# A QKV product on one core: second pair of row tiles loaded, cast and turned one tile at a time, and three smaller reorderings of the opening

## The chip, the core and the metric

The kernel runs on one core of one Trainium2 chip. The metric is the device time of one execution in microseconds, as the median of several runs. The core has TensorE (matrix products; the profile shows its products as PE and its loads of weights as PEld), VectorE (DVE), ScalarE (ACT), GpSimd (POOL) and SyncE (SP, which issues most of the transfers). SBUF is the working memory on the chip, PSUM holds the results of TensorE in eight banks per partition, and the inputs and outputs lie in HBM.

## The reference

```python
def setup_inputs():
    batch, seq, hidden = 16, 512, 768
    return {
        "x": np.random.randn(batch, seq, hidden).astype(np.float32),
        "w_qkv": np.random.randn(hidden, 3 * hidden).astype(np.float32),
    }

def reference(x, w_qkv):
    qkv = np.matmul(x, w_qkv)
    hidden = x.shape[-1]
    q = qkv[..., :hidden]
    k = qkv[..., hidden:2*hidden]
    v = qkv[..., 2*hidden:]
    return np.stack([q, k, v], axis=0).astype(np.float32)
```

It is one product of an 8192 x 768 matrix with a 768 x 2304 matrix, whose columns are split into three outputs.

## The kernel before

**Tiling.** The 8192 rows of x are taken in 32 pairs of row tiles of 128 rows each (`NP` is 32; "pair 0" is the first). The contraction of 768 is cut into six steps of 128 (`KT` 6), named j, or two halves of three steps (`KH` 3). The 2304 columns of w are cut into four blocks of 512 (`CB`) and a remainder of 256 (`REM`). Two blocks make a group q; group 0 holds columns 0 to 1023, group 1 columns 1280 to 2303, and the remainder lies between them.

**Two ways to multiply.** For most pairs, a pair of row tiles and a group of two blocks form a "quad": a 2 x 2 by 2 x 2 block product, done in seven products instead of eight (`product` and `do`, numbered 1 to 7). Products 1 and 2 use bf16 copies (`xb` of x, `b1` of w); products 3 to 7 use sums and differences in fp32r (`s` of x, made in `sums_x`; `t1` to `t4` of w, made by `sum_w`; and `b22`, a rounded copy of the last quarter of w). Pairs 0 and 1 come before these sums exist. Their blocks of columns are multiplied directly in bf16 by `block`, which runs over steps j and over the four row tiles 0 to 3 (tiles 0 and 1 are pair 0, 2 and 3 pair 1). `block(0, 0, ...)` uses the first 512 columns, `block(0, 1, ...)` the second 512. The list `singles` gives the order of j and tiles of the first of these.

**The order is written by hand.** Each engine executes its instructions in the order in which the program issues them, and waits for semaphores where it needs another engine's result. A DMA issued by SP waits until the eighth one before it has landed, so up to eight are on their way. They are taken from one queue in order.

**The opening.** The loads are issued in this order: x of pair 0 (768 KB), x of pair 1 (768 KB), six slices of w's first block (256 KB each, one for each j), w's second block in two transfers of 768 KB, a first part of x of pair 2, the remainder of w (768 KB), the seven other parts of pair 2 (96 KB each), then the blocks of group 1. TensorE first runs ten products of zeros (`busy(10)`, L469). `cast_rows` (by way of `copy_halves`, L165 and L166) rounds a pair's x to bf16, half of each row tile on VectorE and half on ScalarE. `turn_rows` then transposes it on TensorE (L185), six 128 x 128 turns to a row tile, and copies the result out of PSUM (L192 on ScalarE, L194 on VectorE) into `xb`. `cast_j` rounds one 512-column slice of w (L474 on ScalarE, L476 on VectorE). The products of `block` are L496, and its results are copied out of PSUM on ScalarE by the functions that it returns (`late`, L488).

**Pairs 2 and 3.** From pair 2 on, x comes in an order in which VectorE can turn it by itself (`transpose`, L155, in two halves for pairs 2 and 3: first the first row tile, then the second). `round_row` (L214 on ScalarE, L216 on GpSimd) rounds one row tile of a turned pair to bf16, and `sums_x` makes its five sums. After `block(1, 0, ...)` the copies of its results run on ScalarE; then come `sum_w(1, 1)`, `sum_w(1, 2)` (L119), the rounding of `b22[1]` on GpSimd (L621), the turning of pair 3, the rounding of its two row tiles, and its sums. `block(1, 1, ...)` follows. Pair 2's second quad `u2` then runs its products 1 and 2; products 1 of pair 3's two quads follow in `two`; and then `middle(u2)` adds product 6 into the bank that held u2's product 1. That bank has first been copied out by ScalarE (`evacuate`, L267). The products of the quads are L258, those with the remainder of w L321.

**The rest.** A loop takes two pairs at a time (`summed`, `plain`), with loads and turning of later pairs placed between the products. The change doesn't touch it.

Of the kernel before, what the change touches and what calls it, by code (L numbers as in the profile page):

```python
# [10 lines left out]
def kernel(  # L11
# [20 lines left out]
    nc = tc.nc  # L32
    P = 128
# [3 lines left out]
    K = H  # L37
    N3 = w_qkv.shape[1]
    KT = K // P
    KH = KT // 2  # L40
# [8 lines left out]
    bf16 = mybir.dt.bfloat16  # L49
    ident = mybir.ActivationFunctionType.Identity  # L50
# [3 lines left out]
    x_flat = x.rearrange("b t h -> (b t) h")  # L54
# [12 lines left out]
    xb_pool = ctx.enter_context(tc.tile_pool(name="xb", bufs=4))  # L67
    rem_pool = ctx.enter_context(tc.tile_pool(name="rem", bufs=1))
    s_pool = ctx.enter_context(tc.tile_pool(name="s", bufs=2))
    ps_pool = ctx.enter_context(tc.tile_pool(name="ps", bufs=8, space=bass.MemoryType.PSUM))  # L70
# [4 lines left out]
    eye = w_pool.tile([P, 176], bf16, name="eye")[:, :P]  # L75
    w_rem = [w_pool.tile([P, KH, REM], bf16, name="w_rem0"), None]

    b1 = [w_pool.tile([P, KT, CB], bf16, name=f"b1_{q}") for q in range(2)]
# [11 lines left out]
    def load_w(dst, j0, nj, off, cols):  # L90
        rows = w_qkv.rearrange("(p j) n -> p j n", j=KT)
        nc.sync.dma_start(dst, rows[:, j0:j0 + nj, off:off + cols])

    stage = {}

    def load_blocks(q, c, nj=KH):
        if q == 0:
            t = tq_pool.tile([P, KT, CB], fp32, name="st0", tag="tq")
            for j in range(0, KT, nj):
                load_w(t[:, j:j + nj], j, nj, Q_OFF[q] + c * CB, CB)  # L100
            stage[q, 0, c], stage[q, 1, c] = t[:, :KH, :], t[:, KH:, :]
        else:
            for h in range(2):
                if c == 0 and h == 0:
                    t = st_first
                else:
                    t = st_pool.tile([P, KH, CB], fp32, name="st1", tag="st")[:]
                load_w(t, h * KH, KH, Q_OFF[q] + c * CB, CB)
                stage[q, h, c] = t

    def sum_w(q, n):
        t1, t2, t3, t4 = ts[q]
        o, in0, in1 = {
            1: (t1, stage[q, 0, 1], stage[q, 0, 0]),
            2: (t2, stage[q, 1, 1], t1),
            3: (t3, stage[q, 1, 1], stage[q, 0, 1]),
            4: (t4, stage[q, 1, 0], t2),
        }[n]
        nc.vector.tensor_tensor(o, in0, in1, op=sub)  # L119

    xin, xf, xb, sr = {}, {}, {}, {}
# [25 lines left out]
    def transpose(p, parts=1, which=None):  # L147
        if p not in xf:
            xf[p] = xf_pool.tile([P, KT, 2 * P], fp32, name="xf")
        turned = xf[p][:].rearrange("p j (g b) -> p g j b", b=G)  # L150
        rows = xin[p][:].rearrange("p g (a j) -> p g j a", a=G)
        n = 2 * P // G // parts
        for i in range(parts) if which is None else (which, ):
            g = i * n
            nc.vector.transpose(turned[:, g:g + n], rows[:, g:g + n])  # L155

    def load_rows(p):
        xin[p] = xin_pool.tile([P, 2, K], fp32, name="xin")  # L160
        rows = x_flat[p * 2 * P:(p + 1) * 2 * P, :]
        nc.sync.dma_start(xin[p][:], rows.rearrange("(r m) k -> m r k", m=P))  # L162

    def copy_halves(dst, src):
        nc.vector.tensor_copy(out=dst[0], in_=src[0])  # L165
        nc.scalar.activation(dst[1], src[1], ident)  # L166

    xc = {}

    def cast_rows(p):  # L170
        src = xin.pop(p)
        xc[p] = s_pool.tile([P, 2, K], bf16, name="xc", tag="s")
        for r in range(2):
            halves = (slice(0, K // 2), slice(K // 2, K))
            copy_halves([xc[p][:, r, n] for n in halves], [src[:, r, n] for n in halves])

    def turn_rows(p, between=None):
        c = xc.pop(p)
        xb[p] = xb_pool.tile([P, KT, 2 * P], bf16, name="xb", tag="xb")
        turned = []  # L180
        for r in range(2):
            cols = c[:, r, :].rearrange("m (p j) -> m j p", j=KT)
            ps = ps_pool.tile([P, KT, P], bf16, name="ps")
            for j in range(KT):
                nc.tensor.transpose(ps[:, j, :], cols[:, j, :], eye)  # L185
            turned.append(ps)

        def copy(r, h, eng):
            n = slice(h * KH, (h + 1) * KH)
            dst, src = xb[p][:, n, r * P:(r + 1) * P], turned[r][:, n, :]  # L190
            if eng is nc.scalar:
                eng.activation(dst, src, ident)  # L192
            else:
                eng.tensor_copy(out=dst, in_=src)  # L194

        for r in range(2):
            copy(r, 0, nc.vector)
        if between is not None:
            between()
        for r in range(2):  # L200
            copy(r, 1, nc.scalar)

    def round_x(p):
        xb[p] = xb_pool.tile([P, KT, 2 * P], bf16, name="xb", tag="xb")
# [2 lines left out]
    act, dve = nc.scalar, nc.vector  # L207

    def round_row(p, r, eng):
        n = slice(r * P, (r + 1) * P)  # L210
        if r == 0:
            xb[p] = xb_pool.tile([P, KT, 2 * P], bf16, name="xb", tag="xb")
        if eng is act:
            eng.activation(xb[p][:, :, n], xf[p][:, :, n], ident)  # L214
        else:
            eng.tensor_copy(out=xb[p][:, :, n], in_=xf[p][:, :, n])  # L216

    def sums_x(p, eng=None):
        t = xf[p]
        a11, a12 = t[:, :KH, :P], t[:, KH:, :P]  # L220
        a21, a22 = t[:, :KH, P:], t[:, KH:, P:]
        s = s_pool.tile([P, 5, KH, P], f32r, name="s")
        sr[p] = s
        sums = {
            1: lambda g: g.tensor_tensor(s[:, 1], a21, a22, op=add),  # L225
            2: lambda g: g.tensor_tensor(s[:, 2], s[:, 1], a11, op=sub),  # L226
            3: lambda g: g.tensor_tensor(s[:, 3], a11, a21, op=sub),  # L227
            0: lambda g: g.tensor_copy(out=s[:, 0], in_=a22),
            4: lambda g: g.tensor_tensor(s[:, 4], a12, s[:, 2], op=sub),  # L229
        }  # L230
        if eng is not None:
            return sums
        for n in (1, 2, 3, 0, 4):
            sums[n](nc.gpsimd)
# [5 lines left out]
    def quad(p, q, pool=o_pool, tag="o"):  # L240
        u = Quad()
        u.p, u.q = p, q
        u.o = pool.tile([P, 2, 2 * CB], fp32, name="o", tag=tag)
        u.x = u.y = u.z = None
        return u
# [205 lines left out]
    zero = xb_pool.tile([P, CB], bf16, name="zero", tag="xb")  # L451
    nc.vector.memset(zero[:], 0.0)
    load_rows(0)
    nc.scalar.activation(tiny[:], zero[:, :1], ident)
    make_identity(nc, eye)
    load_rows(1)
    load_blocks(0, 0, 1)
    load_blocks(0, 1)
    st_rem = o_pool.tile([P, KT, REM], fp32, name="str", tag="o")
    load_x_rows(2, (0, ))  # L460
    load_w(st_rem[:], 0, KT, R_OFF, REM)
# [3 lines left out]
    def busy(n):  # L465

        ps = bank()
        for _ in range(n):
            nc.tensor.matmul(ps[:], zero[:, :P], zero[:], start=True, stop=True)  # L469

    def cast_j(q, c, w, j, eng=act):
        src = stage[q, j // KH, c][:, j % KH, :]
        if eng is act:
            eng.activation(w[:, j, :], src, ident)  # L474
        else:
            eng.tensor_copy(out=w[:, j, :], in_=src)  # L476
# [55 lines left out]
            round_x(p)  # L532
            sums_x(p)

    singles = [((0, ), (0, 1)), ((1, ), (0, 1)), ((0, 1), (2, 3))]
    singles += [((j, ), range(4)) for j in range(2, KT)]

    busy(10)
    cast_rows(0)
    turn_rows(0, lambda: cast_rows(1))  # L540
    busy(2)
    cast_j(0, 0, b1[0], 0, dve)
    cast_j(0, 0, b1[0], 1, dve)
    turn_rows(1)
    for j in range(2, KT):
        cast_j(0, 0, b1[0], j, dve)
    late0 = block(0, 0, b1[0], singles)
# [70 lines left out]
        f()  # L618
    sum_w(1, 1)
    sum_w(1, 2)  # L620
    nc.gpsimd.tensor_copy(out=b22[1][:], in_=stage[1, 1, 1])  # L621
    transpose(3, 2)
    round_row(3, 0, act)
    round_row(3, 1, nc.gpsimd)
    sums_x(3)
    sum_w(1, 3)
    sum_w(1, 4)
# [25 lines left out]
    for p in range(ND + 3, NP - 1, 2):  # L653
# [16 lines left out]
        c, d = quad(p + 1, 0), quad(p + 1, 1)  # L670
# [34 lines left out]
```

## Time and profile before

| What | Value |
|---|---|
| Time, median of 3 runs | 358.84 us (358.75 to 359.02) |
| Time of the profiled execution | 358.81 us |
| Its span, first to last instruction | 357.0 us |
| PE busy | 350.6 us, 98% of the span, 1757 instructions |
| DVE busy | 264.4 us, 74% |
| ACT busy | 185.0 us, 52% |
| POOL busy | 177.3 us, 50% |
| DMA moved | 108.10 MB, mean 303 GB/s |
| Granted TensorE clock, mean | 1.000 |

Times in the profile are microseconds from the first instruction. The span is what the profile covers; the device time of the same execution is 1.8 us longer. A busy engine is one that has an instruction in progress, and products on PE overlap each other, so "busy" alone doesn't say that nothing could start sooner. A timeline row gives the start, the duration, the engine and line, the operation, the tile written and the tiles read, the shape, and how many instructions were merged; in brackets stands the idle time before it and what ended that. PEld rows are loads of weights: a load is done shortly ahead of its product. The letter q after an engine's name means that engine's sequencer.

### The profile page before, as it was taken

Reading aid. Unit: us, or ns where it says so; the run is one execution under the profiler, and the core shown is the slowest. Engines: PE = TensorE matmul, PEld = TensorE weight load, DVE = VectorE, ACT = ScalarE, POOL = GpSimd, SP = SyncE. Lnnn points to the kernel's source line nnn. Section 1 sums busy time; section 2 is a strip of 40 time slices with the busy share of each in tenths; the row PEclk is TensorE's granted clock in tenths of the full one; section 3 lists DMA queues with packets and bytes.
Section 4 is the critical chain, followed back from the end, with each engine's and each line's share of the span. In section 5 each row is a group of like instructions: output and inputs, shape, how many; then the busy total and the mean of one; then the engine's idle time right before and its main releaser. Section 6 shows DMA issues by size and latency. Waiting matters only on the chain.

```text
span 357.0 us, 5315 instructions
## 1 busy us (share of the span) xinstructions
PE 350.6 (98%) x1757; PEld 252.1 (71%) x1776; DVE 264.4 (74%) x310; ACT 185.0 (52%) x317; POOL 177.3 (50%) x184
## 2 busy tenths in 40 slices
PE   7999999999999999999999999999999999999996
PEld 3474677768677686877768677686877768677674
DVE  3789876796877869777695877869777695876743
ACT  4587754545454553645545454553645545454553
POOL 0031773376566453665535566353665535566320
PEclk9999999999999999999999999999999999999999
DMA  7997999999999898998979899698999979887497
GB/s 296 380 353 238 325 378 340 373 317 348 308 311 340 257 361 206 347 266 285 361 197 385 227 342 307 209 402 213 347 263 307 331 196 392 225 303 280 155 380 260
DMA packets 82075, 108.10 MB, mean 303 GB/s; under 512 B 4992, under 2 KB 62080, under 8 KB 82048
## 3 DMA queue, kind: packets, MB, share of 16 engines
q1 hardware_dynamic: 75088, 102.52, 85.7%
q10 hardware_dynamic: 6960, 5.24, 5.5%
q8 instruction: 14, 0.23, 0.3%
q14 instruction: 13, 0.11, 0.1%
HBM read 32.24 MB, written 75.50 MB: 302 GB/s over the span
## 4 chain that ended last, share of the span: by engine, by line
PE 74%; POOL 15%; DVE 6%; issue 3%; DMA 2%; ACT 0%; SPq 0%
PE ps L258 56%; PE ps L321 12%; PE ps L496 6%; DVE xf L155 6%; POOL xb L205 5%; POOL s L226 3%; POOL s L225 3%; POOL s L227 3%; DMA xin<-in_x_dram 2%; PE ps L185 0%; DVE o L304 0%; ACT xc L166 0%; SPq L162 0%; DVE orem L424 0%; ACT orem L423 0%
## 5 line engine op out<-in xcount | busy, mean ns | idle before, releaser
L258 PE MATMUL ps<-t,s 128*128 128x512 f32 x720 | 177.9, 395 | 0.0
L258 PEld LDWEIGHTS ps<-t,s 128*128 128x128 f32 x720 | 135.1, 188 | 29.5
L155 DVE STREAM_TRANSPOSE xf<-xin 128x768 f32<-128x768 f32 (+1 forms) x45 | 93.3, 2075 | 4.3 <-DMA xin<-in_x_dram 4.3
L258 PE MATMUL ps<-b,xb 128*128 128x512 bf16 x343 | 81.6, 379 | 1.1
L298 DVE TENSOR_TENSOR o<-o,ps 128x512 f32<-128x512 f32 x56 | 38.5, 688 | 50.7 <-ACT o L297 50.0
L205 POOL CAST xb<-xf 128x1536 bf16<-128x1536 f32 x28 | 41.1, 1467 | 56.9 <-DVE xf L155 54.8
L225 POOL TENSOR_TENSOR s<-xf 128x384 fp32r<-128x384 f32 x29 | 31.0, 1068 | 72.9 <-DVE xf L155 71.1
L258 PEld LDWEIGHTS <-xb 128*128 128x128 bf16 x360 | 33.9, 98 | 36.7 <-issue 3.9
L304 DVE TENSOR_TENSOR o<-o,ps 128x512 f32<-128x512 f32 x60 | 41.1, 687 | 20.5 <-PE ps L258 19.4
L297 ACT ACTIVATE o<-ps 128x512 f32<-128x512 f32 x56 | 33.5, 598 | 42.1 <-PE ps L258 42.1
L258 PE MATMUL ps<-b,s 128*128 128x512 f32 x180 | 50.6, 389 | 0.0
L301 ACT ACTIVATE o<-ps 128x512 f32<-128x512 f32 x60 | 35.9, 598 | 25.2 <-PE ps L258 22.8
L378 DVE TENSOR_TENSOR o<-o,ps 128x512 f32<-128x512 f32 x78 | 47.8, 680 | 0.0
L321 PE MATMUL ps<-w_rem,xb 128*128 128x256 bf16 x384 | 47.4, 273 | 0.0
L286 ACT ACTIVATE o<-ps 128x512 f32<-128x512 f32 x60 | 35.9, 599 | 19.4 <-PE ps L258 14.0
L321 PEld LDWEIGHTS <-xb 128*128 128x128 bf16 x384 | 37.3, 98 | 11.5 <-issue 0.5
L335 ACT ACTIVATE orem<-ps 128x512 f32<-128x512 f32 x31 | 18.5, 598 | 48.3 <-PE ps L321 34.0
L258 PEld LDWEIGHTS ps<-b,s 128*128 128x128 f32 x180 | 33.8, 188 | 7.0
L226 POOL TENSOR_TENSOR s<-s,xf 128x384 fp32r<-128x384 f32 x29 | 29.5, 1018 | 2.3
L227 POOL TENSOR_TENSOR s<-xf 128x384 fp32r<-128x384 f32 x29 | 29.4, 1015 | 0.0
L229 POOL TENSOR_TENSOR s<-xf,s 128x384 fp32r<-128x384 f32 x29 | 29.2, 1008 | 0.0
L382 ACT ACTIVATE o<-ps 128x512 f32<-128x512 f32 x26 | 15.5, 598 | 17.9 <-PE ps L258 17.3
(49 smaller groups left out, 161.2 us busy)
## 6 DMA issues: line engine op xcount, KB each, us to landing
out_dram<-o SPq DMA_DIRECT2D x60, 768.0 KB, 4.6
out_dram<-o SPq DMA_DIRECT2D x75, 256.0 KB, 3.8
xin<-in_x_dram SPq DMA_DIRECT2D x88, 192.0 KB, 5.6
out_dram<-orem SPq DMA_DIRECT2D x31, 256.0 KB, 2.2
xin<-in_x_dram ACTq DMA_DIRECT2D x24, 192.0 KB, 4.4
st<-in_w_qkv_dram SPq DMA_DIRECT2D x5, 768.0 KB, 7.9
xin<-in_x_dram SPq DMA_DIRECT2D x2, 768.0 KB, 4.9
st<-in_w_qkv_dram SPq DMA_DIRECT2D x6, 256.0 KB, 6.0
```

What stands on the lines that cost most here:

```text
L155: nc.vector.transpose(turned[:, g:g + n], rows[:, g:g + n])
L205: nc.gpsimd.tensor_copy(out=xb[p][:], in_=xf[p][:])
L225: 1: lambda g: g.tensor_tensor(s[:, 1], a21, a22, op=add),
L226: 2: lambda g: g.tensor_tensor(s[:, 2], s[:, 1], a11, op=sub),
L227: 3: lambda g: g.tensor_tensor(s[:, 3], a11, a21, op=sub),
L258: nc.tensor.matmul(ps[:], lhs[j], rhs[j], start=(start and j == 0), stop=(j == KH - 1), skip_group_check=True,)
L286: nc.scalar.activation(c12, u.x[:], ident)
L298: nc.vector.tensor_tensor(c22, c22, u.y[:], op=add)
L301: nc.scalar.activation(c21, u.x[:], ident)
L304: nc.vector.tensor_tensor(c12, c12, u.y[:], op=add)
L321: nc.tensor.matmul(ps, xb[p][:, j, r * P:(r + 1) * P], w_rem[j // KH][:, j % KH, :], start=(j == 0), stop=(j == KT - 1), skip_group_check= ...
L378: dve.tensor_tensor(c, c, u.z[:], op=add)
```

## The change

Four things are changed, all before the loop.

1. Pair 1's x is loaded by two transfers of 384 KB, one for each row tile, where it was one of 768 KB. Casting and turning go by row tile: the first tile of pair 1 is cast and turned while the second is still on its way. The two filler products (`busy(2)`) stand between the two turns of pair 1.
2. The first slice of w (j = 0) is cast by VectorE (288 columns) and ScalarE (224 columns) where VectorE did it alone. `singles` is shorter: steps j are taken one at a time, j = 0 with tiles 0 and 1, then with tiles 2 and 3, then each other j with all four.
3. w's second block is loaded in six slices of 256 KB, where it was two transfers of 768 KB.
4. Pair 3's first row tile is rounded on GpSimd, ahead of the rounding of `b22[1]`, and its second on ScalarE; before, the first was rounded on ScalarE and the second on GpSimd, after `b22[1]`.

SP issues five more transfers in all; ScalarE gets its part of the first slice and one more copy of turned rows (the first half of the second tile of pair 1); and the order on VectorE changes as the code says.

```diff
-    def load_rows(p):
+    def load_rows(p, parts=(slice(0, 2), )):
         xin[p] = xin_pool.tile([P, 2, K], fp32, name="xin")
-        rows = x_flat[p * 2 * P:(p + 1) * 2 * P, :]
-        nc.sync.dma_start(xin[p][:], rows.rearrange("(r m) k -> m r k", m=P))
...
+        rows = x_flat[p * 2 * P:(p + 1) * 2 * P, :].rearrange("(r m) k -> m r k", m=P)
+        for r in parts:
+            nc.sync.dma_start(xin[p][:, r], rows[:, r])
+
+    xc, turned_rows = {}, {}
+
+    def cast_row(p, r):
+        if p not in xc:
+            xc[p] = s_pool.tile([P, 2, K], bf16, name="xc", tag="s")
+        dst, src = xc[p][:, r], xin[p][:, r]
+        nc.vector.tensor_copy(out=dst[:, :K // 2], in_=src[:, :K // 2])
+        nc.scalar.activation(dst[:, K // 2:], src[:, K // 2:], ident)
+
+    def turn_row(p, r):
+        if r == 0:
+            xb[p] = xb_pool.tile([P, KT, 2 * P], bf16, name="xb", tag="xb")
+        cols = xc[p][:, r, :].rearrange("m (p j) -> m j p", j=KT)
+        ps = ps_pool.tile([P, KT, P], bf16, name="ps")
+        for j in range(KT):
+            nc.tensor.transpose(ps[:, j, :], cols[:, j, :], eye)
+        turned_rows[p, r] = ps
+
+    def copy_row(p, r, h, eng):
+        n = slice(h * KH, (h + 1) * KH)
+        dst, src = xb[p][:, n, r * P:(r + 1) * P], turned_rows[p, r][:, n, :]
+        if eng is nc.scalar:
+            eng.activation(dst, src, ident)
+        else:
+            eng.tensor_copy(out=dst, in_=src)
...
-    load_rows(1)
+    load_rows(1, range(2))
     load_blocks(0, 0, 1)
-    load_blocks(0, 1)
+    load_blocks(0, 1, 1)
...
-    singles = [((0, ), (0, 1)), ((1, ), (0, 1)), ((0, 1), (2, 3))]
-    singles += [((j, ), range(4)) for j in range(2, KT)]
+    singles = [((0, ), (0, 1)), ((0, ), (2, 3))]
+    singles += [((j, ), range(4)) for j in range(1, KT)]
 
     busy(10)
-    cast_rows(0)
-    turn_rows(0, lambda: cast_rows(1))
+    for r in range(2):
+        cast_row(0, r)
+    for r in range(2):
+        turn_row(0, r)
+    cast_row(1, 0)
+    copy_row(0, 0, 0, dve)
+    copy_row(0, 1, 0, dve)
+    copy_row(0, 0, 1, act)
+    turn_row(1, 0)
     busy(2)
-    cast_j(0, 0, b1[0], 0, dve)
+    cast_row(1, 1)
+    turn_row(1, 1)
+    copy_row(1, 0, 0, dve)
+    k0, part = stage[0, 0, 0][:, 0, :], 288
+    dve.tensor_copy(out=b1[0][:, 0, :part], in_=k0[:, :part])
+    act.activation(b1[0][:, 0, part:], k0[:, part:], ident)
+    copy_row(1, 1, 0, act)
     cast_j(0, 0, b1[0], 1, dve)
-    turn_rows(1)
+    for p, r in ((0, 1), (1, 0), (1, 1)):
+        copy_row(p, r, 1, act)
     for j in range(2, KT):
         cast_j(0, 0, b1[0], j, dve)
...
     sum_w(1, 1)
     sum_w(1, 2)
+    transpose(3, 2)
+    round_row(3, 0, nc.gpsimd)
     nc.gpsimd.tensor_copy(out=b22[1][:], in_=stage[1, 1, 1])
-    transpose(3, 2)
-    round_row(3, 0, act)
-    round_row(3, 1, nc.gpsimd)
+    round_row(3, 1, act)
     sums_x(3)
```

More of the change, by code (lines that the diff above doesn't have):

```diff
@@ L155, in transpose @@
             nc.vector.transpose(turned[:, g:g + n], rows[:, g:g + n])
-    def load_rows(p):
+    def load_rows(p, parts=(slice(0, 2), )):
         xin[p] = xin_pool.tile([P, 2, K], fp32, name="xin")
-        rows = x_flat[p * 2 * P:(p + 1) * 2 * P, :]
-        nc.sync.dma_start(xin[p][:], rows.rearrange("(r m) k -> m r k", m=P))
[L164 to L201, printed above, removed]
+        rows = x_flat[p * 2 * P:(p + 1) * 2 * P, :].rearrange("(r m) k -> m r k", m=P)
```

## The prediction

> **What bounds the kernel now.** I read the stretches first (columns: stretch and length in us, then busy time of PE, PEld, DVE, ACT and POOL, granted clock, DMA share, GB/s).
>
> ```profile
> 0.00:8.00 8.00, 6.18 (x31) 2.69 (x32) 2.68 (x8) 3.50 (x7) 0.70 (x6) 1.00 0.76 283
> 8.00:21.00 13.00, 12.95 (x76) 7.07 (x77) 9.89 (x15) 7.03 (x14) 2.62 (x2) 1.00 1.07 366
> 21.00:46.00 25.00, 24.82 (x126) 14.38 (x127) 22.76 (x20) 20.26 (x39) 10.36 (x8) 1.00 0.92 309
> 46.00:343.00 297.00, 295.99 (x1478) 220.20 (x1491) 223.78 (x261) 148.85 (x249) 163.61 (x169) 1.00 0.92 300
> ```
>
> From 8 us on TensorE is busy for practically all of every stretch. A shift that TensorE still has at 46 us reaches the end; nothing after 46 us is changed. So I need two things: how early the products begin, and which instructions up to 46 us would make TensorE wait if it came earlier. Next the chain of waits over the opening, then the timeline of VectorE, ScalarE and TensorE there:
>
> ```profile
> 1.24 5.67 DMA xin<-in_x_dram
> ...
> 6.93 0.53 ACT xc L166
> ...
> 7.51 0.95 PE ps L185 x12
> 8.46 2.82 PE ps L496 x13
> ```
> ```profile
> 4.97 0.94 ACT L166 ACTIVATE xc<-xin 128x384 bf16<-128x384 f32 x2 [2.74 <-DMA xin<-in_x_dram]
> ...
> 6.93 0.63 DVE L165 CAST xc<-xin 128x384 bf16<-128x384 f32 x2
> ...
> 7.57 0.43 DVE L476 CAST b<-st 128x512 bf16<-128x512 f32 x1
> ...
> 8.26 0.43 DVE L476 CAST b<-st 128x512 bf16<-128x512 f32 x1 [0.27 <-DMA st<-in_w_qkv_dram]
> 8.29 5.36 PE L496 MATMUL ps<-b,xb 128*128 128x512 bf16 x23
> ```
>
> The second pair lands at 6.91, is cast, and its twelve turns (7.51 to 8.46) stand in TensorE's order ahead of the first product at 8.29. From there products follow each other every 0.216 us. Later, two places have no slack:
>
> ```profile
> 18.62 3.17 DVE L155 STREAM_TRANSPOSE xf<-xin 128x768 f32<-128x768 f32 x2 [0.78 <-DMA xin<-in_x_dram]
> ...
> 20.27 0.84 ACT L214 ACTIVATE xb<-xf 128x768 bf16<-128x768 f32 x1 [0.96 <-DVE xf L155]
> ...
> 21.18 0.42 PEld L258 LDWEIGHTS <-xb 128*128 128x128 bf16 x3
> ```
> ```profile
> 31.74 1.47 POOL L621 CAST b<-st 128x1536 fp32r<-128x1536 f32 x1 [8.92 <-DMA st<-in_w_qkv_dram]
> 31.78 3.03 DVE L119 TENSOR_TENSOR t<-st,t 128x1536 fp32r<-128x1536 f32 x1 [0.81 <-DMA st<-in_w_qkv_dram]
> ...
> 34.74 3.02 DVE L155 STREAM_TRANSPOSE xf<-xin 128x768 f32<-128x768 f32 x2
> ...
> 36.79 0.88 ACT L214 ACTIVATE xb<-xf 128x768 bf16<-128x768 f32 x1
> ...
> 37.52 2.09 ACT L488 ACTIVATE o<-ps 128x512 f32<-128x512 f32 x4
> ...
> 39.43 1.16 ACT L267 ACTIVATE o<-ps 128x512 f32<-128x512 f32 x2
> ```
>
> Place A: pair 2's first rows land at about 18.5, are turned on VectorE and rounded on ScalarE until 20.27 + 0.84 = 21.11; the load of weights that reads them starts at 21.18. Release to load takes 0.05 elsewhere (cast ends 7.46, turn starts 7.51), so the slack is 0.02. Place B: ScalarE has no idle time from 32.35 on. Its first L267 copy (0.67) ends at 40.10 and frees the bank into which `middle(u2)` accumulates; that load of weights starts at 40.15, so the slack is nothing. In ScalarE's order the rounding at 36.79 stands ahead of four copies and this one.
>
> **The change, part by part.**
>
> *Second pair by row tile.* The load of 768 KB landed 1.96 after the first pair's (4.97 to 6.93), so its first half should land at about 5.95. ScalarE's cast (0.52) ends at 6.49 and six turns run to about 7.1. The second half still lands at 6.91; its ScalarE cast ends at 7.46, and now six turns, not twelve, follow: 7.51 to 7.88, where the next load of weights can start. VectorE does its half casts and copies (0.28 to 0.36 each) in between, with the first pair's copies now behind the cast at 5.97 (they end near 6.9 instead of 6.89), before the 6.93 cast: no cost. The two fillers (L469) move between the two turns.
>
> *First slice cast by two engines.* Slice 0 starts its cast at 7.57, 0.01 after VectorE is free, and so has landed by then. VectorE's 288 of 512 columns take about 0.30 (384 take 0.36, 512 take 0.43), to 7.87; ScalarE's 224 take about 0.38 (384 take 0.52, 512 take 0.63), to 7.95. First product near 8.00 instead of 8.29: a gain of 0.29. What can now be late is the fourth row tile's copy, queued on ScalarE behind this part: 8.08 + 0.48 + 0.05 = 8.61 for a product due at 8.65, so at most 0.02 is lost. Slice 1 (cast 8.26 + 0.43 = 8.69) is now due at 8.87, the later ones land every 0.65 and are used every 0.86. Gain at the end of block one: 0.27 to 0.29.
>
> *Second block by slices.* Six transfers of 256 KB for two of 768 KB, and one more for the second pair: five more on SP's queue, which go past pair 2's rows, the remainder of w and all later loads. SP issues one in 0.44; slices use up 0.65 each, so issuing is no limit. SP is held by the landing of the eighth transfer before; that is now smaller, but eight of 256 KB still cover some 5 us. Is a small transfer slower? Slices 1 and 5 of block one are cast at 8.26 and 10.85, 0.65 a slice; the two 768 KB loads are cast at 12.77 and 14.88, so (14.88 - 10.85) / 6 = 0.67 for as much. Hence pair 2's rows land where they did; bounds 6 x 0.05 = 0.3 either way. The first slice of block two lands near 11.5 and not 12.75, so that block can start at 13.2. The waits behind these slices on ScalarE (slices 1, 3, 5, due at 14.1, 15.8, 17.5) have a microsecond or more.
>
> The Trainium skill, in DMA: Bandwidth & Descriptors, section Bandwidth, has the rule to batch transfers to 1 MiB or more for three quarters of the peak, and its section on one DMA's anatomy gives a constant cost of about 2.0 us for each; five more, were that not overlapped, would be 10 us by an estimate from that page. The rows of 0.65 and 0.67 above do not agree with it here.
>
> What the first three parts give is taken back at place A: TensorE arrives up to 0.29 earlier, but pair 2's rows are bound by their landing. What is left is 0.02.
>
> *Pair 3's rounding.* Before, GpSimd's b22 cast (31.74) held VectorE's subtraction beside it: 3.03 for what takes 1.75 at 29.22. It now comes after row 0's rounding, so that subtraction should end at 31.78 + 1.75 = 33.53. The turning of pair 3 then waits for its first four parts; the fourth landed at 33.87, 7.5 us after its issue at 26.36. With the 0.12 that passed at place A between landing and start, it runs from 34.0 and both halves (3.03 together) end at 37.02. GpSimd rounds row 0 at about 35.6 to 36.4 (half of L205's 1.47), long before it is needed (the seventh of twelve loads of weights that begin at 37.55, one every 0.216: 38.85); b22 follows to 37.8 and is needed at 42.88 (PEld row). It may hold the next subtraction by 0.8, which was held elsewhere before (2.38 at 39.32), and whose result is needed at 42.30 (PEld row): nothing. But ScalarE's rounding now is of row 1, the second half: it starts at 37.05 and not at 36.79. Everything behind it moves by 0.26, the copies and then place B: load of weights at 40.42 instead of 40.15. The 0.02 is lost in this wait too, since ScalarE's chain doesn't depend on it. If the rows land up to 0.3 off, the chain before them (held by a store in the same queue) moves along, so I take 0.27 with bounds 0 and 0.6.
>
> **Sum.** -0.29 at the start, + 0.27 at place A, + 0.29 at place B (the 0.02 that was still ahead, and 0.27 beyond the old time): the end is 0.27 later. Profiled execution: span 357.0 + 0.3 = 357.3, time 358.81 + 0.27 = 359.08; the median is 0.03 above it, so 359.1. That is 0.07%, while about 0.2% (0.72 us) is what a measurement can tell from no change.
>
> **The rivals.**
>
> *No wait at B.* If ScalarE's copies catch up, or the second half is turned by 36.75, only place A counts: 358.84 - 0.02 = 358.8. For it: ScalarE's rate behind the rounding is that of its own work. Against: no idle time to catch up in.
>
> *The start's gain survives.* It needs pair 2's rows 0.25 earlier and B clear: 358.84 - 0.28 = 358.56. Against: DMA share is 1.07 in that stretch, so the queue is full, and the bytes are the same.
>
> *Slower: GpSimd's rounding and VectorE's second half hold each other.* At 35.6 row 0's rounding starts just as the second half does. If that turning waits for it, as the subtraction waited at 31.78, it ends 0.75 later, ScalarE's rounding too, and place B costs 0.27 + 0.75 = 1.02: 359.9. It decides from a delay of 0.45 on. For it: the 3.03. Against: at 44.91 a turning of the whole pair took 3.03 beside GpSimd, as it does alone.
>
> *Slower: one late DMA engine.* In the trace fifteen of sixteen shares of pair 3's fourth part had landed by 31.4 and the last at 33.87; the DMA rate falls to 70 GB/s between 30 and 33. Place B has no slack, so a lag larger by 1.0 (it was 1.2 to 3.4 in the first 50 us) would come out whole: 359.1 + 1.0 = 360.1. A smaller lag gives no more than the rival without a wait. Transfers issued at other moments may change it; none of the rows says which way.
>
> **How the numbers follow.** Forecast 0.44, no wait at B 0.15, gain survives 0.07: within 0.2%, 0.66. The two slower ones 0.10 and 0.18: 0.28. For faster by over 0.2% I have no mechanism, as the start can give at most 0.29: 0.06. Range 358.5 to 360.1, from the surviving gain to the late engine; the forecast's own is 358.9 to 359.5.
>
> **What would show it.** First product near 8.0; a slice of block two cast near 11.5; an idle time of TensorE of about 0.25 ahead of the load that reads pair 2's row 0 (near 21.2), released by ScalarE's rounding; the subtraction at 31.8 in 1.75; ScalarE idle some 0.25 ahead of its rounding near 37.0; a second wait of TensorE, of about 0.27, near 40.4. I am wrong if TensorE waits anywhere else before 46, if the second wait is missing, or if pair 2's rows land at another time than 18.5.

## The result, and the profile after

The kernel after takes 359.65 us (median of 12 runs, 359.04 to 360.23), the kernel before 358.91 in the same comparison (12 runs, 358.68 to 359.59). The ratio is 1.002, with an interval of 1.0012 to 1.0027: slower by some 0.7 us, where 0.27 was forecast. It lies within the whole range of 358.5 to 360.1, but above the forecast's own 358.9 to 359.5.

The profiled execution is the slowest of the twelve: 360.23 us, span 358.4, against 358.81 and 357.0 before. Its stretches (stretch and length in us, then the busy time of PE, PEld, DVE, ACT and POOL, granted clock, DMA share, GB/s):

```profile
8.00:21.00 13.00, 12.76 (x69) 6.55 (x71) 8.64 (x13) 6.94 (x14) 2.62 (x2) 1.00 1.05 334
21.00:46.00 25.00, 24.48 (x127) 14.26 (x128) 22.68 (x21) 19.91 (x38) 10.05 (x8) 1.00 0.93 314
46.00:343.00 297.00, 295.99 (x1478) 220.12 (x1492) 224.24 (x260) 149.43 (x250) 163.92 (x169) 1.00 0.92 300
```

The clock is the same, and TensorE's busy time from 46 us on is the same 295.99 of 297. Between 8 and 21 us the transfers moved 334 GB/s, 366 before. The timeline of the same kernel, at the start (start and duration in us, engine, line, operation, and in brackets the idle time before it with what ended it):

```profile
7.35 0.52 ACT L172 ACTIVATE xc<-xin 128x384 bf16<-128x384 f32 x1 [0.29 <-DMA xin<-in_x_dram]
...
7.92 0.40 PEld L180 LDWEIGHTS <-xc 128*128 128x128 bf16 x6 [0.96 <-ACT xc L172]
...
7.99 0.31 DVE L541 CAST b<-st 128x288 bf16<-128x288 f32 x1
...
8.43 1.02 PE L484 MATMUL ps<-b,xb 128*128 128x512 bf16 x4
```

The second tile of pair 1 can be cast only at 7.35, since it landed at 7.32; the whole pair had landed at 6.91 before. So the first product is at 8.43, and not at the 8.00 of the forecast; before it was at 8.29. Then place A:

```profile
19.79 3.05 DVE L155 STREAM_TRANSPOSE xf<-xin 128x768 f32<-128x768 f32 x2 [0.89 <-DMA xin<-in_x_dram]
21.43 0.84 ACT L202 ACTIVATE xb<-xf 128x768 bf16<-128x768 f32 x1 [1.73 <-DVE xf L155]
...
22.32 0.55 PEld L246 LDWEIGHTS <-xb 128*128 128x128 bf16 x4 [0.52 <-ACT xb L202]
```

It is the chain that the forecast named, rows, turning, rounding, load of weights, but it starts from rows that landed at 19.59 instead of 18.50. The idle time of TensorE's loads is 0.52. Place B, in the timeline of the same kernel:

```profile
32.79 1.76 DVE L119 TENSOR_TENSOR t<-st,t 128x1536 fp32r<-128x1536 f32 x1 [0.77 <-DMA st<-in_w_qkv_dram]
...
35.02 3.06 DVE L155 STREAM_TRANSPOSE xf<-xin 128x768 f32<-128x768 f32 x2 [0.48 <-DMA xin<-in_x_dram]
...
36.74 0.83 POOL L204 CAST xb<-xf 128x768 bf16<-128x768 f32 x1 [12.87 <-DVE xf L155]
37.51 1.47 POOL L625 CAST b<-st 128x1536 fp32r<-128x1536 f32 x1
...
38.11 0.84 ACT L202 ACTIVATE xb<-xf 128x768 bf16<-128x768 f32 x1
...
40.77 1.10 ACT L255 ACTIVATE o<-ps 128x512 f32<-128x512 f32 x2
41.44 0.53 PEld L246 LDWEIGHTS ps<-t,s 128*128 128x128 f32 x3 [0.37 <-ACT o L255]
```

The subtraction takes 1.76 now that GpSimd isn't beside it (3.03 before). GpSimd's rounding at 36.74 stands beside the second half of the turning, and the turning takes 3.06 all the same. ScalarE rounds row 1 at 38.11, the copy that place B waits for follows, and TensorE waits 0.37.

### The profile page after: what moved, and what is told of

The parts are those of the page before. It is cut to its first block, busy times and chain, and to the rows that moved or that the text cites. A ratio compares the mean times of both kernels' runs of the same rounds, so it can differ in the third digit from the quotient of the medians.

```text
span 358.4 us, 5323 instructions
## 1 busy us (share of the span) xinstructions
PE 351.1 (98%) x1757; PEld 252.0 (70%) x1776; DVE 264.0 (74%) x309; ACT 186.2 (52%) x319; POOL 177.3 (49%) x184
## 4 chain that ended last, share of the span: by engine, by line
PE 70%; POOL 15%; DVE 6%; DMA 4%; issue 3%; SPq 1%; ACT 0%; DVEq 0%
PE ps L246 56%; PE ps L309 11%; DVE xf L155 6%; POOL xb L193 5%; POOL s L214 3%; POOL s L213 3%; POOL s L215 3%; DMA st<-in_w_qkv_dram 3%; PE ps L484 3%; DMA xin<-in_x_dram 1%; SPq L92 0%; SPq L163 0%; ACT xb L202 0%; DVE o L292 0%; SPq L137 0%
## 5 line engine op out<-in xcount | busy, mean ns | idle before, releaser
L214 POOL TENSOR_TENSOR s<-s,xf 128x384 fp32r<-128x384 f32 x29 | 30.9, 1067 | 2.3
```

## The experiments

In all tables and sums "the shift in the loop" is by how much ScalarE's instructions of the loop stand later than in the profile of before (nearly constant from some 80 to 350 us; the table has its median), and "the end" is the time from the landing of the last store to the end of the span.

### Each part alone, and the change without part four

`only4` is the kernel before with part four alone, `only3` with part three alone, `only12` with parts one and two; `no4` is the kernel after with part four taken out by the same lines in reverse, and `only12` leaves out part three's line too.

```diff
only4:
-    nc.gpsimd.tensor_copy(out=b22[1][:], in_=stage[1, 1, 1])
     transpose(3, 2)
-    round_row(3, 0, act)
-    round_row(3, 1, nc.gpsimd)
+    round_row(3, 0, nc.gpsimd)
+    nc.gpsimd.tensor_copy(out=b22[1][:], in_=stage[1, 1, 1])
+    round_row(3, 1, act)
only3:
-    load_blocks(0, 1)
+    load_blocks(0, 1, 1)
```

> The kernel before with the fourth part of the change alone (pair 3's first row tile rounded on GpSimd ahead of b22's rounding, the second on ScalarE). Theory one (ScalarE's rounding waits for the second half of the turning, and place B passes that on): +0.27 us, between +0.15 and +0.4; the profile shows ScalarE idle by about 0.25 ahead of that rounding, and TensorE waiting about as long near 40.4. Theory two (all of the change's cost is in its transfers): no difference, and no wait near 40.4.

> The kernel before with the third part alone (w's second block in six transfers of 256 KB, not two of 768 KB). Theory one (transfers of 256 KB cost nothing; a late DMA engine is chance): no difference within 0.15 us, and pair 2's first rows are turned from about 18.6 as before. Theory two (the added transfers make pair 2's rows land later): +0.3 to +0.6 us, with the turning starting 0.3 or more later than 18.6 and TensorE waiting for pair 2's rounding near 21.2.

> The change's first and second part alone (second pair by row tile, first slice of w by two engines), w's second block in two transfers and pair 3's rounding as before. Theory one: products begin about 0.29 us earlier in the profile unless the second pair's second tile lands late, and all but 0.02 of that is lost at place A, so no difference within 0.15 us. Theory two (each added transfer counts, here one): up to +0.1 us. A lone late engine as in the changed kernel's profile (second tile landing 0.5 late) would show as a first product at or after 8.3.

> The changed kernel with its fourth part undone. Theory one: 0.27 us less than the changed kernel, so +0.45 against the kernel before if the rest of the +0.74 is from transfers, and 0.0 if that rest was chance. Theory two: +0.7, as the changed kernel.

Measured, against 358.95 for the kernel before (33 runs, 358.70 to 359.40):

| Kernel | Median, us | Range | Ratio, interval |
|---|---|---|---|
| only4 | 359.03 | 358.84 to 359.47 | 1.0003, 0.9994 to 1.0012 |
| only3 | 359.26 | 359.04 to 359.64 | 1.0009, 1.0000 to 1.0018 |
| only12 | 359.24 | 358.84 to 359.70 | 1.0009, 1.0000 to 1.0018 |
| no4 | 359.57 | 359.02 to 359.94 | 1.0014, 1.0005 to 1.0023 |

Part four alone costs 0.08, which can't be told from nothing. Parts one and two cost 0.29 by the medians and part three 0.31, each with an interval that just reaches 1; the three together cost 0.62, with an interval clear of it. So the part to which I gave the whole loss gives little of it, and the parts that I took for a gain and for nothing give the rest. In the profiles of only3, only12 and no4 pair 2's rows landed at 18.97, 19.01 and 19.12, so my next theory was that added transfers make these rows late.

### Where the rows lose their time, and whether the delay comes through places A and B

`behind` is the kernel after with pair 2's first part issued behind the remainder of w; `a_slack` is the kernel after with the rounding of pair 2's row 0 shared, `ab_slack` the same with both rows of pair 3 rounded on GpSimd; `one_load` is only12 with one transfer for pair 1.

```diff
behind:
-    load_x_rows(2, (0, ))
     load_w(st_rem[:], 0, KT, R_OFF, REM)
-    load_x_rows(2, range(1, 8))
+    load_x_rows(2)
a_slack:
-    round_row(2, 0, act)
+    xb[2] = xb_pool.tile([P, KT, 2 * P], bf16, name="xb", tag="xb")
+    act.activation(xb[2][:, :2, :P], xf[2][:, :2, :P], ident)
+    nc.gpsimd.tensor_copy(out=xb[2][:, 2:, :P], in_=xf[2][:, 2:, :P])
ab_slack, besides:
+    round_row(3, 1, nc.gpsimd)
     nc.gpsimd.tensor_copy(out=b22[1][:], in_=stage[1, 1, 1])
-    round_row(3, 1, act)
one_load:
-    load_rows(1, range(2))
+    load_rows(1)
```

> The kernel after, with the first part of pair 2's rows issued behind the load of w's remainder instead of ahead of it, so that all eight parts follow each other. Theory one (the loss at 14 to 16 us comes from the part with 768-byte packets meeting the start of the remainder load): the rate at 14 to 16 us goes back to 340 GB/s or more, the remainder lands near 17.2 to 17.6, pair 2's first rows near 18.5 to 18.8 and the time falls to 358.9 to 359.2. Theory two (the loss comes with the added transfers, wherever that part stands): the first rows land at 19.0 to 19.6 again and the time stays at 359.5 to 359.8.

> The kernel after, with the rounding of pair 2's row 0 cut in two: j 0 and 1 on ScalarE (about 0.37 instead of 0.84), j 2 to 5 on GpSimd beside it. Theory (the late landing reaches TensorE through place A alone, and pair 3's transfers, which stand behind stores that wait for TensorE, move with it): the wait at place A shrinks by 0.47, to nearly nothing, pair 3's rows land and place B comes 0.3 to 0.5 earlier, and the time falls by about 0.4, to 359.1 to 359.35. Rival (pair 3's landing is set by the DMA queue and not by TensorE): the wait moves from place A to place B, and the time stays at 359.5 to 359.75.

> The kernel of a_slack with pair 3's row 1 rounded on GpSimd as well, ahead of b22, so that ScalarE has 0.84 us less ahead of the copy that place B waits for. Theory (A and B are the only two places through which the landings reach the end): no wait of TensorE at B; the time is that of the start plus what is left at A: 358.9 to 359.15. Rival (a third place is next, among the sums of pair 3 on GpSimd or the subtraction beside the two roundings): 359.2 or more, with a wait of TensorE between 41 and 46.

> The first two parts of the change (row-tile order, first slice of w cast by two engines) with the second pair still loaded in one transfer; nothing else of the change. Theory (the added transfer is what made parts one and two cost 0.29, not their order): pair 2's rows land at 18.5 again and the time is 358.8 to 359.05. Rival (the order of casts, turns and copies costs by itself): 359.15 to 359.3, with waits of TensorE between 8 and 10.

Measured, against 359.01 for the kernel before (34 runs, 358.68 to 359.74):

| Kernel | Median, us | Range | Ratio, interval |
|---|---|---|---|
| behind | 359.38 | 358.97 to 360.25 | 1.0014, 1.0005 to 1.0023 |
| a_slack | 359.63 | 359.18 to 360.67 | 1.0020, 1.0011 to 1.0028 |
| ab_slack | 359.27 | 358.75 to 359.74 | 1.0007, 0.9998 to 1.0016 |
| one_load | 359.49 | 359.41 to 359.55 | 1.0011, 1.0002 to 1.0019 |

**behind** lands between the two theories in time. Its rows landed at 18.95, so moving that part didn't bring them back to 18.50 in this profile.

**a_slack** met the rival. There was no wait at A (rows 19.02), and the delay stood at B instead. Its timeline:

```profile
34.56 3.06 DVE L155 STREAM_TRANSPOSE xf<-xin 128x768 f32<-128x768 f32 x2 [0.47 <-DMA xin<-in_x_dram]
...
37.65 0.84 ACT L202 ACTIVATE xb<-xf 128x768 bf16<-128x768 f32 x1 [0.17 <-DVE xf L155]
...
40.98 1.00 PEld L246 LDWEIGHTS ps<-t,s 128*128 128x128 f32 x5 [0.79 <-ACT o L255]
```

TensorE came earlier and waited 0.79: place B is bound by the landing of pair 3's rows (34.48 here), not by how early TensorE is. **ab_slack** takes the rounding off ScalarE there; no wait is left at A or B, and the time is 0.36 less than a_slack's. It was still 0.26 above before, and above the 359.15 that the theory allowed, with two terms that I hadn't seen yet: a wait for w's remainder (landed 18.16), by which its shift is +0.47 ahead of place A already, and the end, told below.

**one_load** was expected at the time of before and came out 0.48 above it, the tightest of all kernels. Its timeline shows why:

```profile
7.45 0.39 PEld L180 LDWEIGHTS <-xc 128*128 128x128 bf16 x6 [1.04 <-ACT xc L172]
...
8.49 0.39 PEld L180 LDWEIGHTS <-xc 128*128 128x128 bf16 x6 [0.56 <-ACT xc L172]
...
8.87 2.00 PE L484 MATMUL ps<-b,xb 128*128 128x512 bf16 x8
```

With both tiles landing together, the order by row tiles makes ScalarE's cast of the second tile come late, and the first product is at 8.87. The order of part one is good only if its tiles land apart. But one_load's transfers are those of before, one by one, and still pair 2's rows landed at 18.98. That was against the theory that added transfers make them late.

### The same two kernels once more, and the kernel before with room

`before2` and `after2` are the kernels before and after, unchanged, each profiled a second time. `before_slack` is the kernel before with room at three places:

```diff
-    nc.gpsimd.tensor_copy(out=w_rem[1][:], in_=st_rem[:, KH:])
+    dve.tensor_copy(out=w_rem[1][:, :1], in_=st_rem[:, KH:KH + 1])
+    nc.gpsimd.tensor_copy(out=w_rem[1][:, 1:], in_=st_rem[:, KH + 1:])
...
-    round_row(2, 0, act)
+    xb[2] = xb_pool.tile([P, KT, 2 * P], bf16, name="xb", tag="xb")
+    act.activation(xb[2][:, :2, :P], xf[2][:, :2, :P], ident)
+    nc.gpsimd.tensor_copy(out=xb[2][:, 2:, :P], in_=xf[2][:, 2:, :P])
...
-    nc.gpsimd.tensor_copy(out=b22[1][:], in_=stage[1, 1, 1])
     transpose(3, 2)
-    round_row(3, 0, act)
+    round_row(3, 0, nc.gpsimd)
     round_row(3, 1, nc.gpsimd)
+    nc.gpsimd.tensor_copy(out=b22[1][:], in_=stage[1, 1, 1])
```

> The kernel before, unchanged, profiled once more. Theory one (the change makes pair 2's first rows land late): they land at 18.3 to 18.6 again, the remainder of w at 17.0 to 17.3, and the time is 358.7 to 358.9. Theory two (the landing differs from execution to execution, by chance, in this kernel as in the others): they may land anywhere from 18.3 to 19.1, and where they land later than 18.5 by d, TensorE waits d at place A and the execution is longer by d: span 357.0 plus d.

> The kernel after, unchanged, profiled once more. Theory one: pair 2's first rows land near 19.6 again and the second tile of the second pair near 7.3. Theory two: both landings differ from the first profile by 0.2 to 0.6, either way, and the span follows the later one of places A and B.

> The kernel before with room made at the three places where a late landing reaches TensorE, and no other change to its transfers or its start: the rounding of pair 2's row 0 cut between ScalarE (j 0 and 1) and GpSimd (j 2 to 5), a third of the cast of w's second remainder half moved from GpSimd to VectorE, and both rows of pair 3 rounded on GpSimd ahead of b22. Theory (the spread of the kernel before, 358.7 to 359.7, is late landings that come through these places): with some 0.45 of room at each the slow executions go, and nearly all lie within 0.2 of the fastest: median 358.7 to 358.85, highest below 359.2, ratio to before 0.9990 to 0.9996. Rival (the spread is elsewhere, or a fourth place has no room): the same median and the same spread as before, 358.9 to 359.1.

before2 took 359.15 us (span 357.4). Its timeline at place A:

```profile
19.08 3.22 DVE L155 STREAM_TRANSPOSE xf<-xin 128x768 f32<-128x768 f32 x2 [0.87 <-DMA xin<-in_x_dram]
...
20.70 0.84 ACT L214 ACTIVATE xb<-xf 128x768 bf16<-128x768 f32 x1 [1.37 <-DVE xf L155]
...
21.60 0.98 PEld L258 LDWEIGHTS <-xb 128*128 128x128 bf16 x6 [0.40 <-ACT xb L214]
```

And at place B:

```profile
32.81 0.60 ACT L335 ACTIVATE orem<-ps 128x512 f32<-128x512 f32 x1 [2.25 <-DMA out_dram<-orem]
...
40.62 1.00 PEld L258 LDWEIGHTS ps<-t,s 128*128 128x128 f32 x5 [0.27 <-ACT o L267]
```

The unchanged kernel before has the wait at A too, when its rows land at 18.96. It also waits at B, without part four: ScalarE's unbroken work ahead of that copy begins when a store has landed, here at 32.81 and at 32.35 in the first profile. The profile with which I worked showed the rows at 18.50, one draw of several: in the five profiles whose opening has the transfers of before, they landed at 18.34, 18.50, 18.94, 18.96 and 18.98. The groups of runs were on different chips, but the chip doesn't explain this: the medians of the kernel before in the four groups lie between 358.90 and 359.01.

after2 took 359.33 us (span 357.6), and it is nearly the execution of the forecast. Its rows landed at 18.50, as in the first profile of before. Its timeline at the start, at A and at B:

```profile
7.54 0.40 PEld L180 LDWEIGHTS <-xc 128*128 128x128 bf16 x6 [0.56 <-ACT xc L172]
...
8.01 1.48 PE L484 MATMUL ps<-b,xb 128*128 128x512 bf16 x6
...
8.66 0.54 PEld L484 LDWEIGHTS <-xb 128*128 128x128 bf16 x4 [0.34 <-ACT xb L187]
...
18.69 3.05 DVE L155 STREAM_TRANSPOSE xf<-xin 128x768 f32<-128x768 f32 x2 [0.89 <-DMA xin<-in_x_dram]
...
20.32 0.84 ACT L202 ACTIVATE xb<-xf 128x768 bf16<-128x768 f32 x1 [1.29 <-DVE xf L155]
...
21.21 0.98 PEld L246 LDWEIGHTS <-xb 128*128 128x128 bf16 x6 [0.32 <-ACT xb L202]
...
34.15 3.06 DVE L155 STREAM_TRANSPOSE xf<-xin 128x768 f32<-128x768 f32 x2 [0.56 <-DMA xin<-in_x_dram]
...
37.25 0.84 ACT L202 ACTIVATE xb<-xf 128x768 bf16<-128x768 f32 x1 [0.27 <-DVE xf L155]
...
40.58 1.23 PEld L246 LDWEIGHTS ps<-t,s 128*128 128x128 f32 x6 [0.61 <-ACT o L255]
```

The second tile landed at 6.86, the first product is at 8.01, and both forecast waits are there. The rate from 8 to 21 us is 367 GB/s here and 353 in before2, so the 334 of the first profile of after isn't what the change gives in every execution.

**The end.** The shift in the loop of after2 is 0.33, but its span is 0.53 longer. The rest lies behind the last store. Here are SP's semaphore instructions from the landing of the last store on, in the views of the program's last line: engine, operation, count, and durations in ns. The kernel before, from 356.18 on:

```profile
L700 SPq EVENT_SEMAPHORE  x3: 17/17/27, 356.2 to 357.0; - x3
```

only3, from 356.59 on:

```profile
L700 SPq EVENT_SEMAPHORE  x7: 17/28/28, 356.6 to 357.6; - x7
```

after2, from 356.52 on:

```profile
L702 SPq EVENT_SEMAPHORE  x6: 17/28/28, 356.5 to 357.5; - x6
```

At its end SP waits for the semaphores of its transfers one after the other, each instruction starting some 0.06 after the one before when nothing holds it. Of the three in the kernel before, the first is for the last store and the two others are released by TensorE's sequencer, a hand-over that each kernel has. So before, the last store's semaphore is the last of the row; in only3, with four more transfers, four stand behind it, in the kernel after three. The end takes 0.84 in all five profiles that have the transfers of before, 0.88 with one transfer more (only12), 1.09 in only3, and 1.03 in the six profiles that have parts one and three (after, after2, no4, behind, a_slack, ab_slack). All these kernels move the same bytes.

All profiles together (second tile of pair 1, remainder of w, pair 2's first rows and pair 3's first rows: time of landing; all in us):

| Kernel | Second tile | First product | Remainder | Pair 2 | Pair 3 | Shift in loop | The end | Span |
|---|---|---|---|---|---|---|---|---|
| before | 6.91 | 8.29 | 17.26 | 18.50 | 33.87 | 0 | 0.84 | 357.0 |
| before2 | 6.92 | 8.33 | 17.63 | 18.96 | 34.43 | 0.37 | 0.84 | 357.4 |
| before_slack | 6.83 | 8.22 | 17.63 | 18.94 | 33.98 | 0.06 | 0.84 | 357.1 |
| only4 | 6.78 | 8.35 | 17.01 | 18.34 | 33.51 | 0.05 | 0.84 | 357.1 |
| one_load | 6.85 | 8.87 | 17.79 | 18.98 | 34.49 | 0.66 | 0.84 | 357.7 |
| only3 | 6.86 | 8.25 | 17.73 | 18.97 | 34.13 | 0.41 | 1.09 | 357.7 |
| only12 | 7.02 | 8.21 | 17.91 | 19.01 | 33.66 | 0.39 | 0.88 | 357.5 |
| no4 | 7.40 | 8.50 | 18.11 | 19.12 | 34.36 | 0.57 | 1.03 | 357.8 |
| behind | 7.20 | 8.29 | 17.55 | 18.95 | 33.62 | 0.33 | 1.03 | 357.6 |
| a_slack | 6.91 | 8.07 | 17.85 | 19.02 | 34.48 | 0.74 | 1.03 | 358.0 |
| ab_slack | 7.19 | 8.28 | 18.16 | 19.22 | 33.58 | 0.47 | 1.03 | 357.7 |
| after | 7.32 | 8.43 | 18.32 | 19.59 | 34.94 | 1.22 | 1.03 | 358.4 |
| after2 | 6.86 | 8.01 | 17.22 | 18.50 | 34.07 | 0.33 | 1.03 | 357.6 |

only3 and before2 differ by the end alone: rows at 18.97 and 18.96, shifts of 0.41 and 0.37, and 0.25 more at the end. So the end may be most of what part three costs alone.

before_slack took 358.90 (11 runs, 358.73 to 359.20) against 358.96 (15 runs, 358.73 to 359.31), ratio 0.9999 with an interval of 0.9990 to 1.0008. In its profile the room works; this is its timeline, with rows that landed at 18.94:

```profile
19.06 3.23 DVE L155 STREAM_TRANSPOSE xf<-xin 128x768 f32<-128x768 f32 x2 [0.23 <-DMA xin<-in_x_dram]
20.69 0.42 ACT L570 ACTIVATE xb<-xf 128x256 bf16<-128x256 f32 x1 [1.46 <-DVE xf L155]
20.72 0.61 POOL L571 CAST xb<-xf 128x512 bf16<-128x512 f32 x1 [0.56 <-DVE xf L155]
...
21.16 1.02 PEld L258 LDWEIGHTS <-xb 128*128 128x128 bf16 x6
```

The load follows without idle time, where before2 with the same rows waited 0.40. But the median is only 0.06 lower, as the rival had it, and the ratio was expected at 0.9996 or less. That such rows cost nothing here is seen in this one profile; that it shortens the median isn't shown.

### The start's gain with room behind it

`all_room` is before_slack with parts one and two of the change and another order of the first products:

```diff
-    singles = [((0, ), (0, 1)), ((0, ), (2, 3))]
-    singles += [((j, ), range(4)) for j in range(1, KT)]
+    singles = [((0, ), range(3)), ((1, ), range(3)), ((0, 1), (3, ))]
+    singles += [((j, ), range(4)) for j in range(2, KT)]
```

> The kernel of before_slack with the first two parts of the change (second pair in two transfers, first slice of w cast by two engines) and the order of the first products turned so that the fourth row tile comes after six of the others; the second block still comes in two transfers. Theory (the gain at the start is real and reaches the end once the places behind it have room): where the second tile lands near 6.9 the first product stands at 8.0 to 8.05 and nothing waits up to place B, which comes at 39.9 to 40.1; where that tile lands near 7.2 the first product is at 8.2 to 8.3 and nothing is won. Median 358.65 to 358.85, ratio to before 0.9990 to 0.9997. Rival (the added transfer costs as much by later landings as the start gives): first product earlier, waits at the remainder of w or at place A of 0.2 or more, 358.9 to 359.2.

It took 359.38 (11 runs: 358.61 to 359.77, and one execution of 1292.04 us that stands apart; 359.32 without it), against 358.90 (15 runs, 358.79 to 359.29); ratio 1.0009, interval 0.9999 to 1.0018. Its lowest run is the lowest of this study; its median without that execution is 0.42 above before, with an interval that just reaches 1, and above what theory and rival had. Its profile is of an execution of 359.51, and its timeline at the start shows the case in which nothing is won:

```profile
7.37 0.52 ACT L172 ACTIVATE xc<-xin 128x384 bf16<-128x384 f32 x1
...
8.46 1.06 PE L484 MATMUL ps<-b,xb 128*128 128x512 bf16 x4
```

The second tile landed at 7.35 (a transfer's landing is told in sixteen shares, and fifteen had landed by 6.82). The remainder landed at 18.42 (fifteen shares by 17.27) and the shift ahead of place A is 0.67 already; nothing is added at A or B. The rival's waits are there, ahead of place A, but not its earlier product. In both landings it is one share that is late. I found no version that beats the kernel before.

## Why the prediction was right, and where it was off

The direction came out and the size didn't. That the time lies in the whole range is in part luck, since only the rival of a late engine had stretched it to 360.1. What each part gives was wrong: the forecast had -0.02 for parts one to three together and 0.27 for part four, and measured were 0.62 (no4) and 0.08 (only4). Of the signs named in the forecast, after2 has all but the size of the second wait; the first profile of after speaks against it, with waits of the loads at 10.43 and 19.63, ahead of place A, and rows at 19.59.

**The start.** "First product near 8.00 instead of 8.29" holds where the second tile lands in time: 8.01 in after2, 8.07 in a_slack. The step that failed is "the second half still lands at 6.91". In the six profiles above with one transfer for the pair it landed at 6.78 to 6.92; in the eight with two (all_room among them) at 6.86 to 7.40, in six of them later than 7.0. So the gain of 0.29 comes in some executions and turns into a loss of up to 0.21 in others. The fourth row tile's copy cost nothing, as forecast: in after2 TensorE is still 0.27 ahead of before at the first load of weights for the remainder (18.18 against 18.45), in spite of the 0.34 that PEld shows at 8.66. That idle time of the loads held the products up by at most 0.01.

**Place A.** "What the first three parts give is taken back at place A" is what after2 shows: 0.28 ahead at the start, 0.06 ahead behind place A. But "hence pair 2's rows land where they did" took one landing for a fixed time. It differs by some 0.6 among profiles with the same transfers, by 0.46 between two of the kernel before (1.09 between two of the kernel after), and A passes a delay beyond 18.50 on: in the seven profiles that wait at A (before2, only3, only12, no4, behind, after, after2) the load starts 2.64 to 2.73 behind that landing, where the forecast had 2.68.

**Place B.** "It starts at 37.05 and not at 36.79" was forecast for rows that land at 33.87. In after2 they landed 0.20 later, and ScalarE rounds 0.20 later, at 37.25; the load at B was forecast at 40.42 and came at 40.58. The mechanism and its size hold there: from the landing to the load the forecast had 6.55, and it is 6.50 or 6.51 in the three profiles with part four that wait at B (after, after2, a_slack). In only4 the rows landed at 33.51, TensorE didn't wait, and its median is 0.08 above before. So the term of 0.27 is one for late rows, and smaller as a mean.

**The rivals.** GpSimd's rounding and VectorE's turning didn't hold each other: 3.06 beside it, 3.02 before. The late engine came nearest, in another place than I had put it: at the second tile of pair 1 and at pair 2's rows, not only at pair 3's. Whether the waits disappear or the gain survives depends on the landings of each execution, so these weren't rivals of the forecast so much as other draws of it.

**What I had left out.** "Nothing after 46 us is changed" is true of the products and false of the end: 0.19 more behind the last store, in both profiles of after. It belongs to "Is a small transfer slower?", where I had asked what a transfer costs while it moves and not what it leaves behind. The sum that should have stood there, with after2's terms: -0.28 at the start, +0.22 at A, +0.39 at B and past it (a shift from -0.06 to 0.33), +0.19 at the end, +0.52 in all, as 359.33 stands to 358.81. For the first profile of after: +0.13 at the start, +0.50 up to A by late slices and a late remainder, +0.42 at A, +0.17 at B, +0.19 at the end, 1.41 of the 1.42 between 360.23 and 358.81. The measured 0.74 of the medians lies between these two.

The Trainium skill's rule of batching (DMA: Bandwidth & Descriptors, section Bandwidth) speaks against parts one and three; the page measured it, and its cost of 2.0 us for each transfer, on transfers that GpSimd issues, and here SP issues them. In after2 the twelve slices still land one in 0.66 (7.55 to 14.80), so the rule doesn't show as a lower rate there. What goes with the smaller transfers here is the longer end, and a second tile that lands late more often.

**Still open.** Why the second tile lands late when it has a transfer of its own: in after two of the 3072-byte packets of pair 1 took 0.54 and 0.62 us between 5.2 and 6.3, where 0.12 is usual, and after2 has none of these. The five profiles in which that tile landed at 7.19 or later (after, no4, behind, ab_slack, all_room) all have such packets of more than 0.5, and none of the nine others has one above 0.39; what holds them isn't shown. The late share isn't always a single one: in no4 four shares landed between 7.30 and 7.40. And whether more transfers shift the mean landing of pair 2's rows: it is 18.74 over the five profiles with the transfers of before and 19.11 over the nine others (all_room's 19.64 among them), with a spread of 0.6 and 1.1 within the two groups.

## What to carry to other kernels

Take the landing of a transfer from several profiles, not from one, before a chain with 0.02 of slack is called bound: where an engine is busy all the time, early time is lost at the first place that a landing binds, and late time is kept. Before a transfer is split, ask three things: when its last share lands, what its pieces do to the order that assumed them to land apart, and what the program does with one more transfer after its last store. A change whose terms are each 0.2 to 0.3 us is as large as the spread of the landings, so it needs the profile taken twice on both sides.

## What the runs showed of the hardware

- The program's end waits for the semaphores of the transfers in the same order in every profile, some 0.06 us each. How many of these waits come after the last store changes with the number of transfers: none in before (the end takes 0.84 us), one with one transfer more (0.88), four with four more (1.09), three with five more (1.03).
- One of sixteen shares of a transfer can land 0.5 us after the fifteenth (6.83 and 7.32 in after, 6.82 and 7.35 in all_room), and the cast that waits for the transfer starts only then. In all_room the last share stays some 0.5 behind the fifteenth in each of the next six transfers (10.73 and 11.23 in the last of these).
- Two turnings of 128x768 elements on VectorE, the second beside a cast of GpSimd, took 3.06 us, and 3.02 without the cast, while a subtraction beside one took 3.03 instead of 1.76.
